# Splitting the merge weights in other jobs of an encoder layer, and storing the attention's values from GpSimd

## The chip, the core and the metric

The kernel runs on one core of a Trainium2 chip. The metric is the device time of one execution in microseconds (us). Three timed executions of the kernel before gave 2698.85, 2699.50 and 2701.23 us; their median, 2699.5 us, is the time before.

## What is computed

One layer of a hybrid encoder, for a prompt of 1024 tokens and a sample of 2048, both with 16 learned meta tokens in front, in float32 with D = 1024. One projection feeds neighbourhood attention (8 heads of 64), a bidirectional mLSTM (4 heads of 128), and two gates for the merge:

```
xn   = rmsnorm(h) * g_pre
proj = xn @ w_in + b_in           # na q,k,v,z | ml qk,v,z,o,g | merge gates
ya = (attention(q, k, v, rpb) * silu(na_z)) @ w_a
yb = (mlstm(qk, v, g, o) * silu(ml_z)) @ w_b
y  = (sigmoid(ga) * ya + sigmoid(gb) * yb) @ w_out
out = h + rmsnorm(y) * g_post
```

The reference is float32. The kernel multiplies with TensorE's faster float32r format, so every operand is split into a high and a low part, and each product is three matmuls (high x high, high x low, low x high).

## The kernel before

**Two streams of work.** `run` interleaves two generators. The dense one makes the projections and the merges, the sparse one the mLSTM (`ml`) and the attention (`na`) of tokens whose projections are there. TensorE's order is the program's own; on the other engines and on the DMA queues a scheduler orders instructions by a timeline that it estimates when the program is built. SyncE (SP) issues nearly all DMAs, and GpSimd (POOL) some; both are queues in which an issue that waits holds up all behind it.

**Chunks and jobs.** `PLAN` lists the dense stages. Its entries are `(sequence, first token, columns)`: entries 0 and 1 are the prompt's mLSTM and its attention columns with values; entry 2 is `(1, 0, "mv")`, the first long chunk (tokens 0 to 1023 of the sample); entry 3 is `(1, 1024, "mv")`, the second long chunk. Here "m" stands for the mLSTM's columns and "v" for the attention's values. `layout` makes nine jobs of "mv": two column jobs ("fm", four units of 128 feature columns, weights as the stationary operand, `fm_half`, L202 to L204), six token jobs ("tm", tokens as the stationary operand, `tm_unit`, L771 to L773: two for the output gate and the mLSTM's gates, two for the mLSTM's values, two for the attention's values), and one column job last. A token job takes two weight tiles, a column job four. In the profile of before the first long chunk's token jobs run from 567 to 738 us, beside the prompt's mLSTM; the second chunk's from 903 to 1078 us, beside the prompt's attention.

**Weights.** All weights go through `whl`, four tiles of 1 MB (high and low part). `requests` makes one list of keys, in which order `wpump` fills the tiles. A key that is used for the first time is loaded raw (`wraw<-wu`, 512 KB, L274, two or more tiles ahead), split by an ACT copy (L302) and a DVE subtraction (L303), and the two parts are stored (`w<-whl`, L326); later uses load them back (`whl<-w`, 1 MB, L295). The 16 keys of the merges, eight of `w_a` and `w_b` together and eight of `w_out`, are needed only in the final stages. They are split ahead of time (`ahead`): such a key takes a `whl` tile from the time it is split until its store has landed, and no matmul reads it. It counts as one of four tiles until the next `wtake` passes it (`wrdy` holds None for it, `wdone` frees the place). In before one key of `ahead` stands before each job of entries 2 and 3, nine in the first long chunk and seven in the second.

**Values.** In the value jobs VectorE adds the bias on the way out of PSUM (`stT`, L787 for the prompt, L789 for the sample). `tm_store` writes each block of 128 tokens in two DMAs of 64 KB into `NV` (L830): 96 in all, 32 for the prompt and 64 for the sample. Four `stT` tiles are in turn.

**On GpSimd's queue.** `wprep` (L571, L589) loads pairs of column weights (`pr<-wu`), and stores sums of them (`q<-po`); `tprep` (L662) stores combinations of the activations; `nprep` (L603, L618, L619) does for the attention's columns what `wprep` does for others, during the second long chunk. ACT and DVE work between these transfers, in the order of their own queues. The attention loads its masks from this queue, too (L1179).

Of the kernel before, what the change touches and what calls it, by code (L numbers as in the profile page):

```python
# [57 lines left out]
def _weight_units():  # L58

    return ([("i", x, P) for x in FM_COLS] + [("t", *c, a) for c in TM_COLS for a in range(2)]  # L60
            + [("m", f, P) for f in range(KT)] + [("o", c, a) for c in range(4) for a in range(2)])


def _sw_order(pairs):

    seq = [(pairs[0], "11")]
    for i, p in enumerate(pairs):
        mid = ("22", "s1") if i == 0 else ("s1", "22")
        seq += [(p, o) for o in ("12", "s2", "s3") + mid]
        if i + 1 < len(pairs):  # L70
            seq.append((pairs[i + 1], "11"))
        seq.append((p, "s4"))
    return seq
# [64 lines left out]
class K:  # L138
# [656 lines left out]
    def tm_store(self, col, wd, s, n, cnt, tok, st):  # L795
        nc, wp = self.nc, self.wp

        def rows(d, c0, c1, lo):
            return d[lo:lo + n * cnt, c0:c1].rearrange("(a p) c -> p a c", p=n)

        f = col % 512
        if col >= C_MO:
            c0 = col - C_MO
            no = min(wd, 512 - c0)
            if wd > no:
                g = wd - no
                if tok is None:
                    for q in range(2):
                        nc.sync.dma_start(self.GA[q][0:NM, :], st[:n, 0, no:wd])
                else:  # L810
                    nc.sync.dma_start(rows(self.GA[s], 0, g, NM + tok), st[:, :, no:wd])
            if tok is not None:
                nc.scalar.activation(st[:, :, :no], st[:, :, :no], AF.Tanh, scale=0.5)
                nc.sync.dma_start(rows(self.TO[s], c0, c0 + no, tok), st[:, :, :no])
        elif col >= C_MV:
            if tok is None:
                for q in range(2):
                    nc.sync.dma_start(self.MV[q][0:NM, f:f + wd], st[:n, 0, :wd])
            else:
                nc.sync.dma_start(rows(self.MV[s], f, f + wd, NM + tok), st[:, :, :wd])  # L820
        else:
            if tok is None:
                for lo in (8, 40):
                    nc.sync.dma_start(self.NVM[lo:lo + NM, f:f + wd], st[:n, 0, :wd])
            else:
                for a in range(cnt):
                    for r in range(2):
                        row = (tok + a * P) // 64 + r
                        dst = self.NV[s][:, row * 8:row * 8 + 8, f:f + wd]
                        nc.sync.dma_start(dst, st[r * 64:r * 64 + 64, a, :wd])  # L830


    def layout(self, cols):
# [15 lines left out]
    def requests(self):  # L849

        unit = {k: j for j, k in enumerate(_weight_units())}
        ahead = deque([("m", f, P) for f in range(KT)] + [("o", c, a) for c in range(4) for a in range(2)])
        for j, (s, t0, cols) in enumerate(PLAN):
            if s == "f":
                assert not ahead
                keys = [("m", f, P) for f in range(KT)] + [("o", c, a) for c in range(4) for a in range(2)]
            else:
                keys = []
                if "g" not in cols:
                    for kind, c in self.layout(cols):  # L860
                        if j >= 2 and ahead:
                            keys.append(ahead.popleft())
                        keys += [("i", x, P) for x in c] if kind == "fm" else [("t", *c, a) for a in range(2)]
                else:
                    assert not ahead
                    pairs = [p for p in range(14) if "ng"[p > 5] in cols]
                    lead = pairs if (s, t0) not in SW else self.lead(j)
                    keys = [("q", (p, f + "1"), (p, f + "2")) for p in lead for f in "12"]
                    pairs = [p for p in pairs if p not in lead]
                    if pairs:  # L870
                        seq = _sw_order(pairs)
                        keys += [("q", *seq[x:x + 2]) for x in range(0, len(seq), 2)]
            for k in keys:
                if k[0] == "q":
                    self.wreq.append((k, None, KT, P))
                    continue
                nk, w = (KT, P) if k[0] in "im" else (4, k[2] if k[0] == "t" else 256)
                self.wreq.append((k, self.i["wu"][unit[k], :, :nk * w], nk, w))
# [1293 lines left out]
```

## Time and profile before

| | before |
|---|---|
| median of the timed executions | 2699.5 us |
| profiled execution, its own time | 2695.33 us |
| its span, first to last instruction | 2693.5 us |
| mean granted TensorE clock | 0.995 |
| busy: TensorE, VectorE, ScalarE, GpSimd | 98%, 72%, 53%, 5% |
| DMA queues: SyncE's hardware queue, GpSimd's software queue | 708.78 MB, 93.93 MB |

In a row of the profile, `whl<-w` names the tile written and the tensor read, and `L295` the line of the kernel. A wait in brackets behind a row, `[6.93 <-DMA whl<-w]`, is the idle time of that engine ahead of it and what ended it. `SPq` is the issuing of a DMA by SyncE, not its transfer. DMA share is the mean busy share of the 16 DMA engines.

### The profile page before, as it was taken

Reading aid. Unit: us, or ns where it says so; the run is one execution under the profiler, and the core shown is the slowest. Engines: PE = TensorE matmul, PEld = TensorE weight load, DVE = VectorE, ACT = ScalarE, POOL = GpSimd, SP = SyncE. Lnnn points to the kernel's source line nnn. Section 1 sums busy time; section 2 is a strip of 40 time slices with the busy share of each in tenths; the row PEclk is TensorE's granted clock in tenths of the full one; section 3 lists DMA queues with packets and bytes.
Section 4 is the critical chain, followed back from the end, with each engine's and each line's share of the span. In section 5 each row is a group of like instructions: output and inputs, shape, how many; then the busy total and the mean of one; then the engine's idle time right before and its main releaser. Section 6 shows DMA issues by size and latency. Waiting matters only on the chain.

```text
span 2693.5 us, 47059 instructions
## 1 busy us (share of the span) xinstructions
PE 2642.1 (98%) x15928; PEld 2332.7 (87%) x15928; DVE 1942.3 (72%) x5266; ACT 1437.7 (53%) x3388; POOL 139.5 (5%) x322
## 2 busy tenths in 40 slices
PE   9999999998999999999999999999999999999998
PEld 7998897888978999888888888887889898989888
DVE  5656678787766888546686786767478989898954
ACT  5423555554444655546665666655365666656521
POOL 0111100001001122000000000000000000000000
PEclk9999999999999999999999999999999999999999
DMA  9899988799977999979889998899899898998975
GB/s 374 325 331 341 327 285 316 272 341 355 325 247 256 302 320 309 296 241 283 258 267 333 368 306 262 280 337 346 253 330 312 260 310 281 283 304 262 322 245 204
DMA packets 397184, 805.71 MB, mean 299 GB/s; under 512 B 48304, under 2 KB 177280, under 8 KB 393104
## 3 DMA queue, kind: packets, MB, share of 16 engines
q1 hardware_dynamic: 370000, 708.78, 78.9%
q0 software_dynamic: 26944, 93.93, 9.4%
q8 instruction: 126, 2.06, 0.3%
q14 instruction: 114, 0.93, 0.1%
HBM read 548.96 MB, written 253.60 MB: 298 GB/s over the span
## 4 chain that ended last, share of the span: by engine, by line
PE 79%; DMA 11%; DVE 6%; ACT 2%; issue 1%; SPq 0%; POOL 0%; DVEq 0%; ACTq 0%; POOLq 0%
PE pj L202 8%; PE pj L204 8%; PE pj L203 8%; PE pj L966 7%; PE pj L968 7%; PE pj L967 7%; PE pj L771 4%; PE pj L773 4%; PE pj L772 4%; PE pj L1928 3%; PE pj L1927 3%; PE pj L1929 3%; DMA whl<-w 3%; PE sm L1261 3%; PE tr L1246 2%
## 5 line engine op out<-in xcount | busy, mean ns | idle before, releaser
L202 PE MATMUL pj<-xh,whl 128*128 128x512 f32 (+1 forms) x960 | 369.6, 385 | 9.8 <-DMA whl<-w 8.2
L204 PE MATMUL pj<-xh,whl 128*128 128x512 f32 (+1 forms) x960 | 362.0, 377 | 0.3 <-DVE whl L303 0.3
L203 PE MATMUL pj<-xl,whl 128*128 128x512 f32 (+1 forms) x960 | 360.7, 376 | 0.1
L771 PE MATMUL pj<-whl,xh 128*128 128x256 f32 (+1 forms) x1152 | 331.4, 288 | 8.1 <-DMA whl<-w 7.4
L773 PE MATMUL pj<-whl,xl 128*128 128x256 f32 (+1 forms) x1152 | 327.3, 284 | 0.0
L772 PE MATMUL pj<-whl,xh 128*128 128x256 f32 (+1 forms) x1152 | 326.9, 284 | 0.0
L771 PEld LDWEIGHTS pj<-whl,xh 128*128 128x128 f32 x1152 | 219.2, 190 | 9.2 <-DMA whl<-w 7.8
L772 PEld LDWEIGHTS pj<-whl,xh 128*128 128x128 f32 x1152 | 219.1, 190 | 0.2
L1927 PE MATMUL pj<-whl,mh 128*128 128x256 f32 x768 | 218.3, 284 | 0.9 <-DMA whl<-w 0.9
L773 PEld LDWEIGHTS pj<-whl,xl 128*128 128x128 f32 x1152 | 219.1, 190 | 0.0
L202 PEld LDWEIGHTS pj<-xh,whl 128*128 128x128 f32 x960 | 181.4, 189 | 42.5 <-issue 8.3
L1928 PE MATMUL pj<-whl,mh 128*128 128x256 f32 x768 | 216.3, 282 | 0.0
L1929 PE MATMUL pj<-whl,mlo 128*128 128x256 f32 x768 | 215.5, 281 | 0.0
L204 PEld LDWEIGHTS pj<-xh,whl 128*128 128x128 f32 x960 | 181.4, 189 | 35.5 <-DVE whl L303 0.5
L203 PEld LDWEIGHTS pj<-xl,whl 128*128 128x128 f32 x960 | 181.7, 189 | 30.5 <-issue 1.0
L966 PE MATMUL pj<-xh,whl 128*128 128x512 f32 x512 | 206.7, 404 | 1.1 <-ACT pj L983 1.1
L968 PE MATMUL pj<-xh,whl 128*128 128x512 f32 x512 | 202.0, 395 | 0.0
L967 PE MATMUL pj<-xl,whl 128*128 128x512 f32 x512 | 201.0, 393 | 0.0
L1253 DVE TENSOR_TENSOR pts<-tr,pts 96x384 fp32r<-96x384 f32 (+2 forms) x192 | 118.6, 618 | 57.9 <-ACT pts L1248 55.7
L1248 ACT ACTIVATE pts<-tr 96x384 fp32r<-96x384 f32 (+2 forms) x192 | 103.4, 539 | 101.1 <-PE tr L1246 100.4
L202 PE MATMUL pj<-yh,whl 128*128 128x512 f32 x384 | 154.1, 401 | 0.0
L203 PE MATMUL pj<-yl,whl 128*128 128x512 f32 x384 | 151.5, 394 | 0.7 <-DVE yl L1829 0.7
(369 smaller groups left out, 6811.8 us busy)
## 6 DMA issues: line engine op xcount, KB each, us to landing
whl<-w SPq DMA_DIRECT2D x136, 1024.0 KB
whl<-q SPq DMA_DIRECT2D x112, 512.0 KB
w<-whl SPq DMA_DIRECT2D x36, 1024.0 KB
wraw<-wu SPq DMA_DIRECT2D x48, 512.0 KB
gt<-st SPq DMA_DIRECT2D x96, 256.0 KB
tg<-gt SPq DMA_DIRECT2D x96, 256.0 KB
q<-po POOLq DMA_DIRECT2D x26, 512.0 KB, 6.7
xt<-xt SPq DMA_DIRECT2D x24, 512.0 KB
```

The source lines that it names most:

```text
L202: mm(out, ah, bh, start=start, stop=False)
L203: mm(out, ah, bl, start=False, stop=False)
L204: mm(out, al, bh, start=False, stop=stop)
L771: nc.tensor.matmul(o, xh, wh, start=k == 0, stop=False)
L772: nc.tensor.matmul(o, xh, wl, start=False, stop=False)
L773: nc.tensor.matmul(o, xl, wh, start=False, stop=k == KT - 1)
L966: mm(bank, w[:, 0, k], xh[:, k], start=fresh and k == 0, stop=False, skip_group_check=True)
L967: mm(bank, w[:, 0, k], xl[:, k], start=False, stop=False, skip_group_check=True)
L968: mm(bank, w[:, 1, k], xh[:, k], start=False, stop=k == 3, skip_group_check=True)
L1927: nc.tensor.matmul(o, mh[:, k, xs], wh, start=clear > 0 and k == 0, stop=False)
L1928: nc.tensor.matmul(o, mh[:, k, xs], wl, start=False, stop=False)
L1929: nc.tensor.matmul(o, ml[:, k, xs], wh, start=False, stop=clear < 2 and k == KT - 1)
```

## The change

Two edits. In `requests`, the merges' keys of entry 2 now stand before its first three jobs only; in entry 3 none stands before the first job, one before the second, and two before each of the six token jobs, which uses up the 13 that are left. In `tm_store`, the attention's value stores are issued by GpSimd instead of SyncE.

```diff
@@ tm_store
-                        nc.sync.dma_start(dst, st[r * 64:r * 64 + 64, a, :wd])
+                        nc.gpsimd.dma_start(dst, st[r * 64:r * 64 + 64, a, :wd])
@@ requests
-                    for kind, c in self.layout(cols):
-                        if j >= 2 and ahead:
-                            keys.append(ahead.popleft())
+                    for n, (kind, c) in enumerate(self.layout(cols)):
+                        for _ in range(n < 3 if j == 2 else 0 if j < 2 or n == 0 else 2 if kind == "tm" else 1):
+                            if ahead:
+                                keys.append(ahead.popleft())
                         keys += [("i", x, P) for x in c] if kind == "fm" else [("t", *c, a) for a in range(2)]
```

TensorE's order stays as it was. The scheduler orders the other engines anew between the prompt's value jobs and the end of the second long chunk, and in one short stretch after it. Where the diff has one more line, lines of the kernel after it are higher by one.

On SyncE's queue, first long chunk, around the weights of the third token job: before, the second tile of the pair (`whl_7370`; the first, `whl_7007`, stands 17 rows above it, with the store of a split key, `w28`, next to it) comes behind stores of the chunk's activations (`xh`, `xl`), loads for the mLSTM (`raw`, `um`, `va`) and stores of the token job before (`gg`, `to`).

```order
L1411 DMA raw_8003<-mk03_207 128x257
L1600 DMA um_7195<-ud00_265 128x2x128
L1600 DMA um_7197<-ud01_266 128x2x128
L811 DMA gg1_259<-stT_7092 128x2x16
L546 DMA xh1_512_5658<-xh_5595 128x512
L546 DMA xl1_512_5659<-xl_5596 128x512
L814 DMA to1_257<-stT_7092 128x2x248
L1481 DMA va0_2774<-mv0_246 128x2x128
L295 DMA whl_7370<-w13_1434 128x2x1024
```

Now the pair for the same job (`whl_6953` and `whl_6985`) stands nearly together, with no raw load and no store of a split key near it:

```order
L295 DMA whl_6953<-w12_1411 128x2x1024
L1601 DMA um_6965<-ud00_265 128x2x128
L1601 DMA um_6967<-ud01_266 128x2x128
L546 DMA xh1_512_5658<-xh_5595 128x512
L295 DMA whl_6985<-w13_1434 128x2x1024
```

The load that was held back by a split key and the traffic behind it has moved up to its partner.

On SyncE's queue, second long chunk, about the start of the second token job: before, one split key is stored (`w37`), between the loads of the next job's two tiles (`whl_11014`, `whl_11404`).

```order
L295 DMA whl_11014<-w12_1411 128x2x1024
L326 DMA w37_10999<-whl_10996 256x1x1024
L274 DMA wraw_11001<-wu 128x1024
L750 DMA bb_11451<-b_in 128x256
L814 DMA to1_257<-stT_10904 128x2x264
L295 DMA whl_11404<-w13_1434 128x2x1024
```

Now two are stored (`w32`, `w33`), each with the raw load of a later key behind it, ahead of the first of these loads (`whl_11374`):

```order
L326 DMA w32_10975<-whl_10972 256x1x1024
L274 DMA wraw_10977<-wu 128x1024
L750 DMA bb_11430<-b_in 128x256
L814 DMA to1_257<-stT_10867 128x2x264
L326 DMA w33_10982<-whl_10979 256x1x1024
L274 DMA wraw_10984<-wu 128x1024
L811 DMA gg1_259<-stT_10988 128x2x16
L814 DMA to1_257<-stT_10988 128x2x248
L295 DMA whl_11374<-w12_1411 128x2x1024
```

The load of the next job's weights has moved behind both stores and behind the job's first block of results.

On GpSimd's queue, last value job of the prompt: before, it holds the stores of split columns (`q10s`), a memset, and the loads of the next pair (`pr`).

```order
L589 DMA q10s_3677<-po 128x1024
L589 DMA q10s_3679<-po 128x1024
L1408 MEMSET raw 128x1
L589 DMA q10s_3859<-po 128x1024
L589 DMA q10s_3861<-po 128x1024
L571 DMA pr<-wu 128x1024 x2
L589 DMA q_4219<-po 128x1024
```

Now stores of values stand between them:

```order
L589 DMA q10s_3677<-po 128x1024
L589 DMA q10s_3679<-po 128x1024
L830 DMA nv_244<-stT 8x8x256 x4
L1409 MEMSET raw 128x1
L830 DMA nv_244<-stT 8x8x256 x2
L589 DMA q10s_3859<-po 128x1024
L589 DMA q10s_3861<-po 128x1024
L571 DMA pr<-wu 128x1024 x2
L830 DMA nv_244<-stT 8x8x256 x2
L589 DMA q_4219<-po 128x1024
```

Six value stores have come between the two pairs of `q10s`, and two behind the loads of `pr`.

## The prediction

> **What bounds the kernel now.** I read the page first, then TensorE's waits, then the windows, then single rows of the timeline. From the page:
>
> ```profile
> span 2693.5 us, 47059 instructions
> PE 2642.1 (98%) x15928; PEld 2332.7 (87%) x15928; DVE 1942.3 (72%) x5266; ACT 1437.7 (53%) x3388; POOL 139.5 (5%) x322
> PE 79%; DMA 11%; DVE 6%; ACT 2%; issue 1%; SPq 0%; POOL 0%; DVEq 0%; ACTq 0%; POOLq 0%
> ```
>
> TensorE is busy for all but 51.4 us, and its work and its order do not change here. So a gain can only come from idle time in the stages that the change touches, 340 to 1110 us (the three chunks' jobs). TensorE's waits in that window, in us in total, times, longest:
>
> ```profile
> PE pj L202 <- DMA whl<-w: 8.2, 3, 3.5
> PE pj L771 <- DMA whl<-w: 7.4, 2, 6.9
> PE sm L204 <- DVE ktl L1552: 6.8, 3, 3.2
> PE sm L1214 <- DVE yg L1276: 2.1, 2, 1.9
> PE pj L771 <- DVE stT L789: 0.7, 1, 0.7
> ```
>
> The largest are waits for weights read back from memory (whl<-w). Busy time by stage (PE, PEld, DVE, ACT, POOL, granted clock, DMA share, GB/s) for the first long chunk's token jobs, the stretch with its last and the next chunk's first two column jobs, the second long chunk's token jobs, and what follows; the fifth row is a later stage:
>
> ```profile
> 560.00:740.00 180.00, 168.75 (x1351) 166.02 (x1350) 136.25 (x366) 80.97 (x199) 21.75 (x42) 0.97 0.98 346
> 740.00:900.00 160.00, 153.42 (x721) 125.73 (x721) 108.73 (x267) 83.40 (x168) 13.13 (x26) 0.99 0.73 254
> 902.00:1078.00 176.00, 175.09 (x1442) 174.89 (x1443) 142.89 (x349) 94.02 (x195) 37.36 (x68) 0.99 0.94 315
> 1080.00:1200.00 120.00, 119.72 (x608) 100.11 (x607) 62.86 (x169) 60.97 (x133) 0.00 (x0) 1.00 0.83 271
> 2000.00:2400.00 400.00, 397.85 (x2592) 359.57 (x2590) 352.99 (x892) 241.55 (x577) 1.54 (x3) 1.00 0.94 290
> ```
>
> The first row is where TensorE loses time, with the DMA engines at 0.98; the third loses almost nothing, at 0.94. Traffic is what the change moves, out of rows one and two into row three.
>
> **Gain: waits that lose their cause.** In the first long chunk a merge weight goes through the four whl tiles in every job; the change leaves the first three. The rows around the stalls (start, length; in brackets the idle time ahead):
>
> ```profile
> 594.68 0.39 PE L771 MATMUL pj<-whl,xh 128*128 128x264 f32 x1 [0.43 <-DMA whl<-w]
> 599.70 0.51 SPq L326 DMA_DIRECT2D w<-whl  x1
> 621.05 0.97 SPq L295 DMA_DIRECT2D whl<-w  x1
> 629.88 0.58 PE L771 MATMUL pj<-whl,xh 128*128 128x256 f32 x1 [6.93 <-DMA whl<-w]
> 739.89 0.56 SPq L295 DMA_DIRECT2D whl<-w  x1
> 747.90 0.47 PE L202 MATMUL pj<-xh,whl 128*128 128x512 f32 x1 [3.05 <-DMA whl<-w]
> 789.83 0.55 SPq L295 DMA_DIRECT2D whl<-w  x1
> 803.98 0.47 PE L202 MATMUL pj<-xh,whl 128*128 128x512 f32 x1 [3.53 <-DMA whl<-w]
> ```
>
> A split was stored at 599.70; the load behind it left at 621.05, and TensorE stood until 629.88. Without the split between them, all four tiles hold weights of this job and the next, and a load goes out a whole job ahead (the order of SyncE above shows the pair together). The same holds at 747.90 and 803.98. These four stalls sum to 0.43 + 6.93 + 3.05 + 3.53 = 13.9 us. After the long ones the clock was low (busy time, clock, DMA share, GB/s):
>
> ```profile
> 630.00:635.00 5.00, 5.00 (x29) 0.63 0.97 343
> 805.00:810.00 5.00, 5.00 (x16) 0.73 1.03 406
> ```
>
> That is 5 x (1 - 0.63) + 5 x (1 - 0.73) = 3.2 us more. Gain: 17.1 us. What is late next there is VectorE, but at 136.25 of 180 us it has room, and it loses the split too. The gain may be 8 if VectorE's waits take half of it, and is at most 20 if one of the 3.2 us waits for ktl goes as well.
>
> **Cost: the second long chunk's token jobs.** A key costs one raw load, one ACT and one DVE pass, one store:
>
> ```profile
> w<-whl SPq DMA_DIRECT2D x36, 1024.0 KB
> wraw<-wu SPq DMA_DIRECT2D x48, 512.0 KB
> L303 DVE TENSOR_TENSOR whl<-wraw,whl 128x1024 fp32r<-128x1024 f32 x22 | 26.9, 1222 | 7.9 <-ACT whl L302 7.9
> L302 ACT ACTIVATE whl<-wraw 128x1024 fp32r<-128x1024 f32 x22 | 23.1, 1051 | 7.0 <-PE pj L204 5.2 <-PE pj L773 1.6
> ```
>
> That is 1.57 MB a key. Between 902 and 1078 three keys are stored now:
>
> ```profile
> L326 SPq DMA_DIRECT2D w<-whl x3: 556/573/762, 935.6 to 993.7; - x3
> ```
>
> With two in each of the first five token jobs it will be ten, so seven more: 11.0 MB. At the cheapest share per byte of the rows above (0.98 at 346 GB/s, 2.83 us per MB) that is 31 us of DMA. Now 0.94 x 176 = 165 us are used: 196 us of work in 176, 20 us too much. Some of it can slip behind 1078, where the next row has a share of 0.83, 20 us free: the last column job's weights are 4 MB (12 us) that are issued up to 31 us ahead of use. I take 10 us as the cost, the middle between 0 (all of it slips or packs) and 20.
>
> VectorE gets 7 x 1.22 = 8.5 us more: (142.9 + 8.5) / 176 = 86%. The fifth row above has 88% and leaves TensorE idle for 2.2 of 400 us, so I take nothing for it; without that cover it would be the 8.5 us.
>
> **The tile chain there.** Both keys use the two tiles that the job does not compute from, so the next job's weights wait until both splits have been stored. Rows for its links, with starts of the first and second job and of the column job after the sixth:
>
> ```profile
> 903.02 0.28 PE L771 MATMUL pj<-whl,xh 128*128 128x264 f32 x1
> 933.43 0.28 PE L771 MATMUL pj<-whl,xh 128*128 128x264 f32 x1
> 935.56 0.56 SPq L326 DMA_DIRECT2D w<-whl  x1
> 942.97 0.56 SPq L295 DMA_DIRECT2D whl<-w  x1
> 1078.10 0.39 PE L202 MATMUL pj<-xh,whl 128*128 128x512 f32 x1
> ```
>
> A job lasts (1078.10 - 903.02) / 6 = 29.2 us. The chain: 2.1 us from a job's start to its store (933.43 to 935.56), 1.2 for the second split, 7.4 until the load can leave (935.56 to 942.97), 8.0 until it lands (739.89 to 747.90): 18.7 us, no stall. With the slow values, 21.4 (599.70 to 621.05) and 14.2 (789.83 to 803.98), it is 38.9, and each of five boundaries stands for 9.7 us. The store of 935.56 is from this very stage, so I add nothing and keep the slow end for the rival.
>
> **GpSimd's stores.** 96 stores of attention's values leave SyncE's queue. SyncE spends 96 x 0.58 = 56 us on them, but carries 0% of the chain, so I count no gain; bounds: 0 and the 0.7 us of TensorE's wait for stT.
>
> ```profile
> L830 SPq DMA_DIRECT2D nv<-stT x96: 570/582/1692, 351.6 to 1079.6; - x96
> 394.41 1.05 POOL L589 DMA_DIRECT2D q10s<-po  x2 [14.68 <-DVE po L563]
> 404.59 1.06 POOL L571 DMA_DIRECT2D pr<-wu  x2
> 411.33 1.06 ACT L585 ACTIVATE po<-pr 128x1024 fp32r<-128x1024 f32 x1 [3.86 <-DMA pr<-wu]
> ```
>
> On GpSimd each now waits for its block's evacuation by VectorE, and behind it stand stores of split columns, loads of the next (pr, xr) and the masks. ScalarE waits for pr at 411.33. Only a pair of value stores stands ahead of that load, 1.06 us at the 0.53 us of an issue; the load has been waiting for other things until 404.59, so the pair is hidden. Cost 0, at most 1 us for each of the two last value jobs of three chunks, 6 us. The Trainium skill, "DMA: Bandwidth & Descriptors", section "Issuing engines are not separate DMA queues", says that such a move saves only the sequencer's time, since the same 16 DMA engines carry all. Here that time is the 56 us above; the rule by itself gives nothing for TensorE, as I take it, and leaves the 11.0 MB where they are.
>
> **Sum.** Against the profiled execution, 2695.3 us (span 2693.5): -17.1 + 10 = about -7 us. That execution lies 4.2 us below the median, 2699.5; from the median I get **2692 us**.
>
> **Rivals.** (1) The gain without the cost: the window packs, -17 us, 2682. For it: 20 free microseconds behind 1078. Against it: the 1.05 share that it needs.
> (2) No change: VectorE takes back half of the gain, -8.5 + 10, about 2701. For it: the 6.8 us of ktl waits.
> (3) Slower: the tile chain. It loses more than the stages before gain from 17.1 / 5 = 3.4 us a boundary, that is a chain over 32.6 us. At 35 us it costs 5 x 5.8 = 29 us, +12, 2711. For it: 21.4 us between a store and its load happened at a share of 0.98, and this stage goes above that. Against it: 7.4 us in the same stage, at 0.94.
> (4) Slower: GpSimd. If an issue waits out a VectorE instruction of 1.2 us, 32 stores in two jobs take 32 x 1.75 = 56 of 58 us, and the column loads behind them are late: half of it, 28 us, gives 2710. Against it: 0.53 us an issue while VectorE is at 76 to 81%. The Trainium skill, "SBUF — State Buffer", section "SBUF: two separate sides", has such a lock between VectorE's two-port modes and the writing of descriptors on GpSimd; the rows of 0.53 us do not show it.
>
> **How the numbers follow.** A difference under 0.2% (5.4 us) is about what a measurement of this kernel cannot tell from none. Forecast 0.40, (1) 0.10, (2) 0.20, (3) 0.25, (4) 0.05. The forecast lies only 2 us beyond the bound, so I give a quarter of it away, half to the same and half to slower; of (2), 0.03 goes to slower and 0.05 to faster. Faster 0.30 + 0.10 + 0.05 = 0.45, same 0.05 + 0.12 = 0.17, slower 0.05 + 0.03 + 0.30 = 0.38. Range: from 2680, rival (1) with 2 us more, to 2718, rival (3) at a chain of 36.4 us; outside it lie the higher half of (3) and little else. The forecast's own range is 2682 to 2702.
>
> **What would show it.** Right: no whl<-w wait of TensorE between 560 and 810, a DMA share of 0.9 or less there; in the second long chunk's token jobs a share over 1.0 and 5 to 15 us of new idle time or slack used up. Wrong: waits of L771 for whl<-w at each token job's start there (rival 3), waits for ktl in the first chunk (2), GpSimd's issues over 1 us (4), or a stall-free second chunk (1).

## The result, and the profile after

The changed kernel takes 2695.07 us (median of 20 executions) against 2699.61 us for the kernel before beside it (20): a ratio of 0.9981, 95% interval 0.9973 to 0.9988. That is 4.5 us faster, about 0.2%, where 7 had been forecast. Timed once more it came to 2695.54 us and 0.9979 (0.9967 to 0.9991). Of all executions timed for this text, one of an experiment below took 6081.75 us; the ratios leave it out.

The profiled execution of the changed kernel took 2696.86 us, 1.8 us above its median; that of before lay 4.3 us below its own. So the two traces differ by +1.5 us where the medians differ by -4.5. They serve to show where time moved, and the medians say how much was left. From the page and TensorE's waits between 340 and 1110 us, after:

```profile
span 2694.8 us, 47090 instructions
PE 2642.9 (98%) x15928; PEld 2334.2 (87%) x15928; DVE 1942.1 (72%) x5266; ACT 1439.8 (53%) x3388; POOL 196.0 (7%) x418
PE pj L771 <- DMA whl<-w: 17.2, 3, 8.3
PE sm L204 <- DVE ktl L1553: 5.9, 5, 2.6
PE sm L202 <- ACT kth L1552: 1.9, 1, 1.9
```

Before, token jobs waited 7.4 us for their weights and column jobs 8.2. Now column jobs wait for none, and token jobs 17.2 us. The timeline of TensorE after: the start of the first long chunk's last column job, the start of the second chunk's first token job, its waits, and the start of the last column job:

```profile
727.16 0.39 PE L202 MATMUL pj<-xh,whl 128*128 128x512 f32 x1
881.26 0.28 PE L771 MATMUL pj<-whl,xh 128*128 128x264 f32 x1
891.20 0.59 PE L771 MATMUL pj<-whl,xh 128*128 128x264 f32 x1 [8.34 <-DMA whl<-w]
955.93 0.39 PE L771 MATMUL pj<-whl,xh 128*128 128x256 f32 x1 [3.73 <-DMA whl<-w]
1019.85 0.58 PE L771 MATMUL pj<-whl,xh 128*128 128x256 f32 x1 [5.13 <-DMA whl<-w]
1078.07 0.40 PE L202 MATMUL pj<-xh,whl 128*128 128x512 f32 x1
```

The second chunk's token jobs start at 881.26 instead of 903.02: 21.8 us gained, more than the 17.1 forecast. They end where they ended before (1078.07, before 1078.10). Six jobs took 175.1 us before and take 196.8 now, so 21.7 us are lost again. Busy time, clock, DMA share and GB/s for the first chunk's token jobs, the column jobs behind them, and the second chunk's token jobs:

```profile
560.00:725.00 165.00, 161.10 (x1313) 158.99 (x1312) 126.93 (x351) 73.93 (x190) 38.38 (x71) 0.99 0.92 326
740.00:880.00 140.00, 140.00 (x664) 115.14 (x663) 100.74 (x247) 73.76 (x143) 13.24 (x26) 1.00 0.71 242
881.00:1077.00 196.00, 178.67 (x1436) 177.56 (x1435) 144.93 (x347) 99.59 (x203) 47.73 (x86) 0.96 0.92 322
```

The first two rows are cured (clock 0.99 and 1.00 where it was 0.97 and 0.99). The third has the damage, at a DMA share of 0.92, which is lower than before (0.94). What the waits cost beyond themselves shows in the granted clock of the five microseconds behind each:

```profile
891.00:896.00 5.00, 4.80 (x26) 4.76 (x27) 3.93 (x9) 0.59 (x1) 0.00 (x0) 0.61 1.00 380
956.00:961.00 5.00, 5.00 (x30) 5.00 (x31) 2.33 (x4) 0.08 (x1) 0.00 (x0) 0.66 1.03 404
1020.00:1025.00 5.00, 5.00 (x24) 4.97 (x25) 1.32 (x4) 0.27 (x1) 1.23 (x2) 0.54 1.03 405
```

That is 5 x (0.39 + 0.34 + 0.46) = 6.0 us. With 17.2 us of waits it makes 23.2, which is 1.5 us more than the loss of 21.7. A second trace of the changed kernel, of an execution of 2695.66 us, shows the same: its token jobs of the second chunk start 22.6 us earlier than before, take 196.1 us, and wait 16.8 us for weights.

### The profile page after: what moved, and what is told of

Its sections match the earlier page's. It is cut to its first block, busy times and chain, and to the rows that moved or that the text cites. A ratio compares the mean times of both kernels' runs of the same rounds, so it can differ in the third digit from the quotient of the medians.

```text
span 2694.8 us, 47090 instructions
## 1 busy us (share of the span) xinstructions
PE 2642.9 (98%) x15928; PEld 2334.2 (87%) x15928; DVE 1942.1 (72%) x5266; ACT 1439.8 (53%) x3388; POOL 196.0 (7%) x418
## 4 chain that ended last, share of the span: by engine, by line
PE 86%; DMA 6%; DVE 5%; ACT 1%; issue 1%; SPq 0%; DVEq 0%; ACTq 0%
PE pj L202 10%; PE pj L204 10%; PE pj L203 9%; PE pj L967 7%; PE pj L969 7%; PE pj L968 7%; PE pj L771 4%; PE pj L773 4%; PE pj L772 4%; PE pj L1929 3%; PE pj L1928 3%; PE pj L1930 3%; PE sm L1262 2%; DMA whl<-w 2%; PE tr L1247 2%; DMA wraw<-wu 1%
## 5 line engine op out<-in xcount | busy, mean ns | idle before, releaser
L202 PE MATMUL pj<-xh,whl 128*128 128x512 f32 (+1 forms) x960 | 369.7, 385 | 2.9 <-ACT whl L302 2.3
L204 PE MATMUL pj<-xh,whl 128*128 128x512 f32 (+1 forms) x960 | 361.4, 376 | 0.3 <-DVE whl L303 0.3
L203 PE MATMUL pj<-xl,whl 128*128 128x512 f32 (+1 forms) x960 | 360.3, 375 | 0.1
L771 PE MATMUL pj<-whl,xh 128*128 128x256 f32 (+1 forms) x1152 | 332.1, 288 | 17.3 <-DMA whl<-w 17.2
L771 PEld LDWEIGHTS pj<-whl,xh 128*128 128x128 f32 x1152 | 220.0, 191 | 18.7 <-DMA whl<-w 18.3
L204 PEld LDWEIGHTS pj<-xh,whl 128*128 128x128 f32 x960 | 181.3, 189 | 35.7 <-DVE whl L303 0.5
L202 PEld LDWEIGHTS pj<-xh,whl 128*128 128x128 f32 x960 | 181.3, 189 | 34.7 <-ACT whl L302 3.2
L203 PEld LDWEIGHTS pj<-xl,whl 128*128 128x128 f32 x960 | 181.7, 189 | 30.6 <-issue 1.0
L202 PE MATMUL pj<-yh,whl 128*128 128x512 f32 x384 | 154.1, 401 | 0.0
L203 PE MATMUL pj<-yl,whl 128*128 128x512 f32 x384 | 151.5, 394 | 0.7 <-DVE yl L1830 0.7
```

The source lines that it names most:

```text
L202: mm(out, ah, bh, start=start, stop=False)
L203: mm(out, ah, bl, start=False, stop=False)
L204: mm(out, al, bh, start=False, stop=stop)
L771: nc.tensor.matmul(o, xh, wh, start=k == 0, stop=False)
```

## The experiments

Two questions are open: whether the tile chain or the traffic made the second chunk slower, and what each edit does by itself. Ratios are to the kernel before, timed beside each kernel.

### The two edits apart

Only the new places of the keys (`tm_store` as before):

```diff
-                        nc.gpsimd.dma_start(dst, st[r * 64:r * 64 + 64, a, :wd])
+                        nc.sync.dma_start(dst, st[r * 64:r * 64 + 64, a, :wd])
```

> Only the new places of the merges' keys; the values are stored from SyncE as before. Theory A (the stores' queue is worth nothing): the same time as the changed kernel, 2695 us, within 1.5 us, and the same three waits of L771 for whl<-w in the second long chunk's token jobs, 15 to 19 us in sum. Rival B (SyncE's queue, shorter by 96 issues, let weights leave earlier, and so part of the 21.8 us gained up to the second chunk's token jobs is the stores' doing): 2698 to 2703 us, with waits for whl<-w back in the first chunk's token jobs. Rival C (the stores cost time on GpSimd's queue): 2690 to 2693 us.

Measured: 2686.89 us, ratio 0.9956 (0.9942 to 0.9970): 8 us faster than with both edits, outside the ranges of all three.

Only the stores on GpSimd, keys as before:

> Only the value stores are moved to GpSimd; the merges' keys stand where they stood before. Theory A: as before, 2699.6 us within 1.5 us, with the waits of before (6.9, 3.1 and 3.5 us for whl<-w between 560 and 810 us) in their places. Rival B: 2693 to 2697 us, with those waits shorter. Rival C: 2702 us or more.

Measured: 2691.35 us, 0.9968 (0.9956 to 0.9980), 8.2 us faster than before. Theory A, which was the prediction's "cost 0, no gain", has fallen. Rival B has the direction here, with more than its range, but of the waits that were to get shorter only the one of 3.05 us at 747.90 went; 6.93 became 6.28 and 3.53 became 4.18. The two gains, 12.6 and 8.2 us, are 20.8 together, of which the changed kernel keeps 4.5.

One part of the stores' gain shows on SyncE's timeline. Before, at the end of the first long chunk's token jobs (two rows of value stores; the weight loads among them left at 739.89, 743.72 and 747.83):

```profile
737.32 2.52 SPq L830 DMA_DIRECT2D nv<-stT  x4
...
740.54 3.08 SPq L830 DMA_DIRECT2D nv<-stT  x4
743.72 0.62 SPq L295 DMA_DIRECT2D whl<-w  x1
...
747.83 0.56 SPq L295 DMA_DIRECT2D whl<-w  x1
```

With only the stores moved, the loads there, and TensorE's start in the same column job:

```profile
727.92 0.53 SPq L295 DMA_DIRECT2D whl<-w  x1
733.26 0.53 SPq L295 DMA_DIRECT2D whl<-w  x1
735.04 1.26 SPq L295 DMA_DIRECT2D whl<-w  x1
734.49 0.39 PE L202 MATMUL pj<-xh,whl 128*128 128x512 f32 x1
```

The loads leave 10 to 13 us earlier, where TensorE is 3.7 us ahead, and the wait of 3.05 us at 747.90 is gone, with the merges' keys where they always were. In the order of the queue the weight loads stood behind value stores. In these rows the stores held them up by being issued rather than by waiting for VectorE: the four from 737.32 end at 739.84, and the load leaves 0.05 us later; the next four end at 743.62, 0.1 us before the next load. Eight issues took 5.6 us, against 4.7 at the median of 0.58 us each. How much of the queue's delay is waiting for VectorE elsewhere was not measured.

The queue explains only this part. This trace reaches the second chunk's token jobs at 897.44, 5.6 us before the kernel before. Of these, 3.05 us are the wait at 747.90 and 1.65 the one at 464.10, which is gone too; but between 436 and 462 us no value store stands on SyncE's queue in either kernel, so there it was the scheduler's new order. A wait for `ktl` at 687.26 is 1.61 us instead of 3.16, and the wait at 803.98 is 0.65 us longer.

### Chain or traffic

The keys of the second chunk are split in a tile of their own; the four whl tiles hold weights alone:

```diff
+            own = self.kp if key[0] in "mo" and raw is not None else None
-            both = wp.tile([P, 2, 4 * WU], F32R, name="whl", bufs=NBW)
+            both = own.tile([P, 2, 4 * WU], F32R, name="wk", bufs=1) if own else wp.tile([P, 2, 4 * WU], F32R, name="whl", bufs=NBW)
...
                     self.hold.append((d, both[:, :, :n].bitcast(F32)))
...
+                if own:
+                    self.wload()
+                    continue
```

> The changed kernel, but in the second long chunk the merges' keys are split in an SBUF tile of their own, so that all four whl tiles hold weights that TensorE reads. The keys' traffic (raw loads and stores), their ACT and DVE passes and their places in the list stay. Theory D (the tile chain: a weight must wait until a key split in its tile has been stored): the three waits of 8.3, 3.7 and 5.1 us vanish (less than 3 us left in sum), and with the low clock behind them 2673 to 2678 us. Rival E (traffic: the DMA engines cannot carry the weights in time whichever tile they go to): 10 us or more of the waits stay, 2690 to 2697 us.

Measured: 2673.2 us, 0.9901 (0.9886 to 0.9915). No wait of TensorE for whl<-w is left in the token jobs; the waits view between 340 and 1110 us (the kernel's lines stand lower here, L203 and L205 for L202 and L204) and the row of the token jobs:

```profile
PE sm L205 <- DVE ktl L1559: 5.6, 5, 2.6
PE sm L203 <- ACT kth L1558: 2.1, 1, 2.1
PE pj L203 <- DMA whl<-w: 1.4, 1, 1.4
881.00:1055.00 174.00, 173.93 (x1446) 173.65 (x1445) 139.18 (x343) 94.24 (x197) 45.52 (x81) 1.00 0.93 316
```

This is what theory D asked for, but it is not clean. With a free tile the scheduler moved keys ahead: six of the thirteen were stored during the token jobs, ten in the changed kernel. So the keys were then held back, each split issued behind the work of its own job:

```diff
-for _ in range(n < 3 if j == 2 else 0 if j < 2 or n == 0 else 2 if kind == "tm" else 1):
+for _ in range(n < 3 if j == 2 else (0, 0, 1, 1, 2, 2, 2, 2, 3)[n] if j == 3 else 0):
...
+                with self.behind() if own else nullcontext():
                     for a in range(parts):
```

> The own SBUF tile again, with the keys held back. With the own tile alone only six of the thirteen keys were stored during the second chunk's token jobs, the others had moved ahead of them; the changed kernel stores ten there. So the stretch lost 4 x 1.57 = 6.3 MB, 18 us of DMA at 2.83 us per MB, and the chain and the traffic were not told apart. Here each split is issued behind the work of its own job, and ten or eleven keys are stored in the stretch, each through the own tile. Theory D (the tile chain): the traffic is that of the changed kernel, and still less than 3 us of waits of L771 for whl<-w are left; the six token jobs take 173 to 178 us, the kernel 2672 to 2678. Rival E (traffic): 0.93 x 174 + 18 = 180 us of DMA work in 174 us; 8 us or more of these waits are back, the six jobs take 183 to 195 us, the kernel 2683 to 2694.

Measured: 2687.34 us, 0.9951 (0.9938 to 0.9965). Nine keys were stored in the token jobs, and the total falls into rival E's range, but the place does not. The token jobs' row, and the two long waits of this kernel, which lie behind the last column job (L974 and L975 are the attention's columns):

```profile
881.00:1056.00 175.00, 174.10 (x1444) 173.46 (x1443) 139.13 (x343) 97.67 (x200) 45.11 (x80) 1.00 1.00 344
1128.53 0.77 PE L974 MATMUL pj<-t1h,whl 128*128 128x512 f32 x1 [8.08 <-DMA t1h<-t01h]
1130.93 0.80 PE L975 MATMUL pj<-t1l,whl 128*128 128x512 f32 x1 [1.63 <-DMA t1l<-t01l]
```

In the token jobs the DMA engines are busy all the time (1.00, 344 GB/s), and still no matmul waits for a weight. With a DMA share higher than the changed kernel's and nearly its keys (nine against ten), without the chain, the jobs take 174.7 us. So this traffic alone does not make the 17.2 us; it takes the chain. What the chain does shows on SyncE's timeline ahead of the first token job: in the changed kernel each of the job's two loads stands behind the store of a key, and the first one waits 3.0 us until that store has landed,

```profile
863.76 0.57 SPq L326 DMA_DIRECT2D w<-whl  x1
869.13 0.33 SPq L295 DMA_DIRECT2D whl<-w  x1
869.55 1.04 SPq L326 DMA_DIRECT2D w<-whl  x1
873.78 0.32 SPq L295 DMA_DIRECT2D whl<-w  x1
```

and in the kernel with the own tile alone the same two loads leave earlier (its L297 is the changed kernel's L295):

```profile
860.54 0.32 SPq L297 DMA_DIRECT2D whl<-w  x1
867.43 0.32 SPq L297 DMA_DIRECT2D whl<-w  x1
```

From the second to the sixth job the own tile's loads leave about as the job before starts, the second of each pair 27 to 29 us ahead. In the changed kernel the load that TensorE waited for left 7.5, 3.8 and 12.3 us before its job started. Traffic has a part in how long such a late load takes: those of the first and the fifth job were used 17.4 and 19.5 us after they left, at DMA shares of 1.02 and 1.05 in the time between. How the 17.2 us divide between leaving late and landing slowly was not measured.

What was pushed out of the stretch in the kernel with the keys held back came back behind it: the combinations of the activations (t1h) were loaded at 1115.45, in the kernel with the own tile alone at 1091.88. Whether the traffic did that, or the last two keys (stored at 1067 and 1085) by holding the SBUF that those tiles take over, was not separated. (When its turn on SyncE's queue came, the late load left 0.27 us behind the issue ahead of it, so it was its place in the queue that was late.)

### Other places for the keys

Keys moved into the first chunk's beginning and the second's column jobs:

```diff
-for _ in range(n < 3 if j == 2 else 0 if j < 2 or n == 0 else 2 if kind == "tm" else 1):
+for _ in range(2 if j == 2 and n < 3 else (1, 2, 2, 1, 1, 1, 1, 1, 0)[n] if j == 3 else 0):
```

> The changed kernel with the 16 keys in other places: two before each of the first three (column) jobs of the first long chunk, none before its token jobs; in the second long chunk one, two and two before the column jobs and one before each of the first five token jobs. Theory D: with one key in a token job only one of its two weights waits for a store, so less than 3 us of waits for whl<-w are left in the second chunk's token jobs; if the column jobs take the moved keys without waits, 2674 to 2680 us. Rival E: five fewer keys lie in the token jobs' stretch, 7.9 MB or 22 us of DMA at the 2.83 us per MB used before, so the waits vanish too; E and D are told apart by the other kernel, not by this one. Rival F (the column jobs cannot take two keys): waits of L202 for whl<-w or of L204 for ktl of 5 us or more between 420 and 570 or 740 and 880 us, 2685 us or more.

That text places them wrongly: only the first two jobs of a chunk are column jobs, and the third is its first token job. So that one has two keys in both chunks, and the following five of the second chunk one each.

Measured: 2697.81 us, 0.9992 (0.9983 to 1.0001), no better than before. Rival F is right on the column jobs, and the one token job with two keys shows the chain again. The waits between 340 and 1110 us, and the row of the second:

```profile
PE pj L202 <- DMA whl<-w: 12.8, 3, 5.7
PE pj L771 <- DMA whl<-w: 8.4, 2, 6.3
905.79 0.59 PE L771 MATMUL pj<-whl,xh 128*128 128x264 f32 x1 [6.30 <-DMA whl<-w]
```

6.3 us stand at the second weight tile of the first token job, the one with two keys. In the five jobs with one key each nothing waits for weights.

Ten keys ahead, one in each job, and the other six split at their first use in the final stages:

```diff
+for _ in range(n < 3 if j == 2 else 0 < n < 8 if j == 3 else 0):
...
+                    self.rest = set(ahead)
...
-                if key[0] in "mo":
+                if key[0] in "mo" and key not in self.rest:
```

> The changed kernel with ten of the merges' keys split ahead: three in the first long chunk as in the change, and one before each of the second to eighth job of the second. The other six are split at their first use, in the first of the final stages. Theory D (tile chain): one key in a token job costs no more than before, so less than 4 us of waits for whl<-w in the token jobs; the final stage gets 6 x 1.22 = 7.3 us of VectorE and 6 x 1.06 = 6.3 us of ScalarE and loses 6 loads of 1 MB for as many raw loads and stores, at a DVE share of about 0.75. If that is hidden: 2674 to 2679 us. Rival (the first use in the final stage is on the path, some 2 us a key): 2684 to 2690 us.

Measured: 2674.43 us, 0.9902 (0.9887 to 0.9917), inside the range of theory D. Its waits between 340 and 1110 us have none for whl<-w:

```profile
PE sm L205 <- DVE ktl L1556: 5.9, 5, 2.6
PE sm L203 <- ACT kth L1555: 2.1, 1, 2.1
PE sm L1218 <- DVE yg L1280: 2.1, 2, 1.9
```

None ahead (the loop over `()`):

> The changed kernel without any key split ahead: all 16 are split at their first use, in the first of the final stages. No key takes a whl tile in the two long chunks, and 16 x 1.57 = 25 MB leave them. The first final stage gets 16 x 1.22 = 19.5 us of VectorE and 16 x 1.06 = 17 us of ScalarE, and 16 raw loads and stores (25 MB) for 16 loads (17 MB). If that stays hidden there, as six keys did: 2671 to 2675 us, no faster than ten ahead, since that one had no whl<-w wait left either. Rival (16 are too many: TensorE waits for the split, some 1 us a key): 2680 to 2690 us.

Measured: 2685.54 us, 0.9950 (0.9938 to 0.9963): the rival. The first final stage waits for ScalarE's split,

```profile
1977.95 0.79 PE L203 MATMUL pj<-yh,whl 128*128 128x512 f32 x1 [4.13 <-ACT whl L305]
2000.00:2100.00 100.00, 97.18 (x668) 89.83 (x667) 90.96 (x215) 68.36 (x155) 1.02 (x2) 0.98 1.03 344
```

and behind it the DMA share stands at 1.03. That wait is only part of the loss: from the last column job of the second long chunk to the end this trace takes 12.7 us longer than the one with ten ahead, and the rest, in shorter waits up to about 2150 us and low clock, was not followed. Six splits at first use are hidden, sixteen are not.

### Why the two edits take from one another

Both were timed again on one chip:

> The changed kernel again, to stand beside its half without the GpSimd stores on one chip. If the two edits really take from one another (each alone gained 8 to 13 us, both together 4.5), it comes out at 2693 to 2697 us, with 14 us or more of waits of L771 for whl<-w in the second chunk's token jobs.

Measured: 2695.54 us, with 16.8 us of waits of L771.

> Only the new places of the merges' keys, again. If the two edits take from one another: 2684 to 2690 us, and a profile near that median has less than 14 us of waits of L771 for whl<-w in the second chunk's token jobs. If the difference between the two kernels was one of chips: 2693 to 2697 us, like the changed kernel.

Measured: 2688.14 us, 0.9954 (0.9937 to 0.9970), with 10.7 us of waits in a profile of 2686.67 us. (The first profile of this kernel, with 17.0 us, was of its longest execution, 2694.55 us.) So the 7 to 8 us came out twice; the intervals of the two kernels lie apart the first time and just overlap the second. The traces show a place. SyncE between the splits' stores and the second load for the third token job, without the GpSimd stores:

```profile
925.96 0.56 SPq L326 DMA_DIRECT2D w<-whl  x1
932.05 0.97 SPq L295 DMA_DIRECT2D whl<-w  x1
934.83 0.57 SPq L295 DMA_DIRECT2D whl<-w  x1
```

and in the changed kernel, with the first and last of the ten rows that stand between its two loads:

```profile
924.28 0.56 SPq L326 DMA_DIRECT2D w<-whl  x1
930.56 1.02 SPq L295 DMA_DIRECT2D whl<-w  x1
935.55 0.50 SPq L1163 DMA_DIRECT2D stk<-nq  x1
...
943.80 0.77 SPq L1150 DMA_DIRECT2D gt<-rpb  x1
945.89 0.58 SPq L295 DMA_DIRECT2D whl<-w  x1
```

The second load leaves 2.8 us behind the first there, and 15.3 us here, where attention's loads and the token job's stores stand in between. It is used at 955.93, after the wait of 3.73 us. The scheduler set this order, and two kernels tell whether the second chunk's stores or the earlier ones bring it about:

```diff
-nc.gpsimd.dma_start(dst, ...)
+(nc.sync if s and tok >= 1024 else nc.gpsimd).dma_start(dst, ...)   # first of the two
+(nc.gpsimd if s and tok >= 1024 else nc.sync).dma_start(dst, ...)   # second
```

> The changed kernel with the values of the second long chunk stored from SyncE; those of the prompt and of the first long chunk stay on GpSimd. Theory J (what the two edits take from one another is SyncE's order in the second chunk: the loads of the second token job's two weights stand 11 places apart in the changed kernel, with attention's loads and stores that wait in between, and 2 places apart where the values are stored from SyncE; the scheduler sets that order before any value of that chunk is stored): here they stand 11 apart, so 2693 to 2697 us, with a wait of 2.5 us or more at the third token job. Rival K (the second chunk's value stores on GpSimd are late themselves or hold up its queue): 2685 to 2689 us.

Measured: 2692.7 us, 0.9974 (0.9962 to 0.9987), with 15.9 us of waits, 2.5 of them at the third token job.

> The counterpart: only the values of the second long chunk are stored from GpSimd, those of the prompt and of the first long chunk from SyncE. Theory J: the two loads stand 2 places apart, so 2685 to 2690 us, with a wait under 1 us at the third token job. Rival K: 2693 to 2697 us.

Measured: 2687.75 us, 0.9955 (0.9941 to 0.9968), with 10.3 us of waits and none at the third token job. Both fit theory J, the first 0.3 us below its range: the time goes with the order that the earlier stores bring about, not with the second chunk's stores. Two things keep this short of proof. The intervals of the two kernels overlap a little, and the profiles are of a short execution of the first (2689.75 us) and of the longest of the second (2692.39 us). And the third job's wait is not the whole difference. The fifth job waits some 5 us in three profiles with the one order; with the other it waits 6.2 us in one profile and not at all in two, where the fourth waits 2.5 to 2.7 us instead. That was not followed.

The own tile with the values stored from SyncE:

> The own SBUF tile for the second chunk's keys, with the values stored from SyncE as before. Theory G (the stores' gain is that SyncE's weight loads no longer stand behind stores that wait for VectorE; with both edits it is given back at the tile chain): without the chain the stores on SyncE cost time again, 3 to 8 us more than the 2673.2 us with GpSimd, 2676 to 2682, with whl<-w waits near 460 us or in the column job after the first long chunk's token jobs. Rival H (GpSimd's stores cost some 8 us themselves once the keys stand in the second chunk): 2664 to 2670 us.

Measured: 2674.84 us, 0.9908 (0.9894 to 0.9923), against 0.9901 with GpSimd: 1.6 us of medians apart, and the intervals overlap. Neither theory G (3 to 8 us) nor rival H got its number. Once keys and weights no longer share tiles, the queue of the value stores makes no difference that was measured, though the wait near 460 us is there again (3.63 us).

The own tile (2673.2 us) and ten keys ahead (2674.4 us) beat both kernels; they lie 26 and 27 us below the kernel before, run beside it. The second needs no more SBUF.

## Why the prediction was right and wrong

**The time.** 2695.1 us lies in the range, and 3 us above the forecast. The sign and the two places were right. That the total came so near is partly luck: two terms were both too small, and the errors went against each other. At the job starts of the traces there is a gain of 21.8 us instead of 17.1, and a cost of 21.7 instead of 10; the medians keep 4.5 of it. That is less than the 5.4 us below which the prediction would have seen no change; with 20 executions of each kernel the interval tells it from none.

**The gain.** The four waits went, as the steps said, and so did the low clock. One step gave at best half of the cause: the wait at 747.90 was put down to a merge weight, but it goes as well when only the value stores leave SyncE's queue and the merges' keys stay. The excess also has the waits at 464.10 (1.65 us) and for `yg` (1.9 us), which the sum did not hold.

**GpSimd's stores, "I count no gain".** This term failed most clearly: alone they are worth 8.2 us. The step that failed was to read SyncE's 0% of the chain as "nothing waits for this queue". The chain books such a wait on the load (`DMA whl<-w`), and the queue in which the load stood behind other issues does not appear in it. The row that told it was on record, with the load at 739.89; what stood ahead of it was not looked at. Not all of the 8.2 us is shown to be this: of the 5.6 us that the trace is ahead at the second chunk's token jobs, 3.05 are. The Trainium skill's "DMA: Bandwidth & Descriptors", section "Issuing engines are not separate DMA queues", counts the saving as the sequencer's time to initiate a DMA, which it calls usually small relative to the DMA itself. The rows at 739.89 show a saving of that kind, 0.58 us a store; what the prediction missed is that a load leaves later by every such issue that stands ahead of it. Rival (4), GpSimd blocked by VectorE, did not occur: 96 issues took 0.58 us each.

**The cost, "half of 20 us of DMA work slips".** The 20 us come near the 21.7 us that were lost, but for the wrong reason, and the 10 us taken of them are less than half. The forecast had 196 us of DMA work in 176 us; the changed kernel's stretch had 0.92 x 196 = 180. The DMA share over 1.0 that was to show it did not come over the stretch. And the own tile with the keys held back shows that the DMA engines can be busy for all of 175 us while TensorE waits for no weight there.

**The tile chain, rival (3).** This is what happened, on a smaller scale than its price. The forecast added up the fast links, 18.7 us, "since the store of 935.56 is from this very stage". But that row had one key in a job. The link that was most too short is the last: instead of 8.0 us from a load's leaving to its use, it was 17.4 at the first job (873.78 to 891.20) and 19.5 at the fifth (1000.35 to 1019.85). At the third job it was another, which the sum did not hold: SyncE's order put the second load 15.3 us behind the first, with other tensors' issues between. Three of the boundaries broke, for 17.2 us, and the low clock behind them, which the gain's sum had and the cost's sum had not, added 6.0. The two kernels with an own tile have none of these waits, and the kernel with two keys in a single token job has one at that job.

**VectorE.** Right in that the token jobs do not wait for it. The share of 86% did not come: 144.93 of 196 us (74%) here, and with the own tile, where the jobs do not stall, 139.18 of 174 (80%) with six keys and 139.13 of 175 with nine.

**What the traces carry.** The second chunk's start moved by 17.7 (value stores of the first chunk on SyncE) to 22.8 us (on GpSimd) with the new places of the keys; what a kernel keeps of that is decided in its token jobs: 196.8 us with both edits, 187.2 with the keys alone (second profile), 173.4 with the own tile.

## What to carry to other kernels

A chain that gives a DMA queue 0% does not say that the queue is free: look at what stands ahead of the late load on its queue, and what that waits for. Where preparatory work borrows buffers from a pool that feeds the bottleneck, price the slowest links that the trace has (store landing, then load landing), not the ones from a stretch that borrowed less; in the second chunk's token jobs one borrowed tile of four cost no wait for weights and two cost 17.2 us of waits, 21.7 us in all; in the first chunk's, one already went with a wait of 6.93 us. And two edits that each gain can share a bound, so time them apart before keeping both.

## What the runs showed of the hardware

A DMA share of 1.00 over 175 us (344 GB/s) left TensorE without a wait for weights, while 0.92 came with 17.2 us of them: how early each load could leave decided, not the share. And a long wait cost some 2 us more in clock, with little regard to its length: behind the 3.7 us the granted clock of five microseconds was 0.66 (1.7 us lost), behind 8.3 us 0.61 (1.9 us) and behind 5.1 us 0.54 (2.3 us). In the traces of all these kernels every wait of TensorE of more than 3.3 us was followed by a low clock (0.50 to 0.71 over five microseconds). Shorter ones were in some cases and not in others. In the kernel before, the five microseconds behind the wait of 3.05 us at 747.90 had the full clock, and those behind a wait of 3.25 us at 441.03 had not:

```profile
748.00:753.00 5.00, 5.00 (x26) 4.19 (x27) 2.40 (x7) 2.01 (x7) 0.00 (x0) 1.00 1.02 341
441.00:446.00 5.00, 4.97 (x20) 4.22 (x21) 3.87 (x6) 3.36 (x7) 0.00 (x0) 0.66 0.86 289
```
